# Slots of stationary activations and high weights start at different remainders of 256 bytes

## The chip, the cores and the metric

The kernel runs on one core of a Trainium2 chip. The metric is the device time of one execution in microseconds (us); the time before is the median of three runs. A core has TensorE (the matrix engine, PE in the profile; its weight loads are PEld), VectorE (DVE), ScalarE (ACT), GpSimd (POOL) and the queue of SyncE (SP). Operands of a matmul lie in SBUF, 128 partitions of some 224 KiB each; an address here is the byte offset within a partition. A matmul first loads its stationary operand (a weight load) and then streams its moving operand past it; the result goes to PSUM.

## The reference

One decoder block, all in float32, with 256 positions and a model width of 2048:

```python
a = rmsnorm(h, norm_mix_pre)
proj = a @ w_in                        # 2048 x 17408
q_a, k_a, v_a, q_r, f_r, i_r, g_r, gate_a, gate_r = split_columns(proj)
attn = ...   # rotary, three groups of dilated windowed attention, mixed by softmax of their log-sums
r_out = ...  # gated linear recurrence in chunks of 64, rmsnorm per head, silu(g_r)
y = sigmoid(gate_a) * (attn @ w_attn_branch) + sigmoid(gate_r) * (r_out @ w_hgrn_branch)
h = h + rmsnorm(y @ w_mix_out, norm_mix_post)
a = rmsnorm(h, norm_ffn_pre)
gt, up = split(a @ w_ffn_gate_up)      # 2048 x 11264
h = h + rmsnorm((silu(gt) * up) @ w_ffn_down, norm_ffn_post)   # 5632 x 2048
```

## The kernel before, in words

Float32 products are made from two-part numbers. Every weight tile is loaded into `raw`, split into a high part (`w`, rounded by ScalarE) and a low part (the rest, by VectorE), and every activation likewise; a product is the sum of high x high, high x low and low x high, each a matmul in the type fp32r. `split` (L282) and `split_wide` (L320) do this for weights, the class `Split` (L429) for activations.

Weights come in an order written out by hand: `seq` is a list of steps, grouped in blocks (L286 to L329), and the main loop (L343) takes one step at a time. It splits the weights of the step after next (`AHEAD` is 2), issues the load three units ahead on the SP queue (`load_behind`, L274), multiplies, and lets pieces of other work (evacuations, attention, recurrence) run between steps as generators. Operations stand on each engine in program order.

There are three kinds of blocks:

- "N" (`multiply`, L296): activations are stationary (128 x 128), 512 columns of weights move. One step has 12 matmuls: two halves of the positions, two row tiles, three products. High and low weights are the two halves of one `w` slot.
- "Wide" (`multiply_wide`, L351): the same roles, 1024 columns of weights per step and 24 matmuls, or, in steps marked 1 in the order, seven products of 2 x 2 blocks instead of eight, 21 matmuls, with sums of weights (`w`, `wl`, `dh`, `dl`) and sums of activations (`so`). Here the low weights have tiles of their own, `wl`.
- "W" (`multiply` too): weights are stationary, the activations xT move: the high weight against 512 columns (high and low part side by side), the low weight against 256. Used for the forget, query and attention projections.

Where operands lie: `rslot` (L110) hands out 16 slots of 1024 elements (4096 bytes) in turn, tag "r"; each holds two row tiles of an activation, high and low. xT, yT, hT, recT and attnT, the sums `so` and the split activations `a` of the last product live there. `wslot` (L279) hands out three slots of 2048 elements (8192 bytes), tag "w". All pool sizes in front of them are such that every one of these slots, and of `raw`, `wl`, `dh` and `dl`, begins at an address whose remainder by 256 is 192. Within a slot, stationary blocks begin at multiples of 512 bytes, moving ones in the "N" and "Wide" blocks at multiples of 2048.

SBUF is full: the last tile ends 64 bytes below 224 KiB. `kp` is a pool that lives through the early and the middle stage; `pool["now"]` is the pool of the present stage alone (early, middle, late; `enter`, L177). `gainr` (4 KiB, L202) is the gain of the recurrence's norm; it is loaded in `opening` (L582) and read by `evac_g` (L750) early on.

The spacing of matmuls comes from the one helper that issues them:

```python
    def mm(ps, lhsT, rhs, start, stop):
        nc.tensor.matmul(ps, lhsT, rhs, start=start, stop=stop, skip_group_check=True)
```

`lhsT` is the stationary operand and is loaded anew for each matmul; all of these matmuls have line L132 in the profile.

Of the kernel before, what the change touches and what calls it, by code (L numbers as in the profile page):

```python
# [13 lines left out]
F32 = mybir.dt.float32  # L14
F32R = mybir.dt.float32r
# [4 lines left out]
P = 128  # L20
# [6 lines left out]
HW = 1024  # L27
# [13 lines left out]
N_RAW, N_SPLIT, AHEAD, WARM, BRIDGE = 3, 3, 2, 8, 6  # L41
# [49 lines left out]
def tile_hybrid_block(ctx: ExitStack, tc: tile.TileContext, t, out):  # L91
# [4 lines left out]
    stream = ctx.enter_context(tc.tile_pool(name="stream", bufs=1, reuse_waits="tile"))  # L96
    rpool = ctx.enter_context(tc.tile_pool(name="rpool", bufs=1, reuse_waits="tile"))
# [3 lines left out]
    dram = ctx.enter_context(tc.tile_pool(name="dram", bufs=1, space=bass.MemoryType.DRAM))  # L101
    ctx.enter_context(tc.manual_schedule())

    serial = [0]

    def nm(s):
        serial[0] += 1
        return f"{s}_{serial[0]}"

    def rslot(s):  # L110
        return rpool.tile([P, 1024], F32R, tag="r", bufs=16, name=nm(s))

    def hslot(s):
        return hpool.tile([P, 2, 512], F32, tag="h", bufs=4, name=nm(s))
# [60 lines left out]
    pool = {}  # L175
# [13 lines left out]
    kp = stage.enter_context(tc.tile_pool(name="kp", bufs=1, reuse_waits="tile"))  # L189
# [9 lines left out]
    cs = kp.tile([P, 2, S], F32, name="cs")  # L199
    amask = kp.tile([P, 2, 512], F32, name="amask")  # L200
    lmask = kp.tile([P, len(LEVELS), 64], F32, name="lmask")
    gainr = kp.tile([P, HW], F32, name="gainr")  # L202
    tabs = kp.tile([P, 4, S], F32, name="tabs")
    bounds = kp.tile([P, 64], F32, name="bounds")
    lb, lb1 = bounds[:, :8], bounds[:, 8:16]


    blocks, seq, units = [], [], []

    def add(*args, **kw):  # L210
        b = Block(*args, **kw)
        blocks.append(b)
        for c in range(b.steps):
            if c % 2 == 0:
                units.append([])
            seq.append(Step(b, c, len(units) - 1, c % 2))
            units[-1].append(seq[-1])
# [59 lines left out]
            load(st.unit + N_RAW, half)  # L277

    def wslot():  # L279
        return stream.tile([P, 2048], F32R, tag="w", bufs=N_SPLIT, name=nm("w"))  # L280

    def split(st, only=None):  # L282
        if type(st.block) is Wide:
            split_wide(st)
            return
        raw = st.raw  # L286
        if st.parts is None:
            w = wslot()
            st.parts = w[:, :1024], w[:, 1024:]
        wh, wl = st.parts  # L290
        for n, k in enumerate(parts(st)):
            if only in (None, n):
                nc.scalar.activation(wh[:, k], raw[:, k], AF.Copy)  # L293
                nc.vector.tensor_sub(wl[:, k], raw[:, k], wh[:, k].bitcast(F32))  # L294
# [25 lines left out]
    def split_wide(st):  # L320

        b, raw = st.block, st.raw
        m, by7 = b.order[st.i]
        prep = b.prep(m, by7) if b.prep else iter(())
        next(prep, None)
        hi, lo = wslot(), p3("wl", F32R, 2048, 3)
        if not by7:
            nc.scalar.activation(hi, raw, AF.Copy)  # L328
            next(prep, None)  # L329
            nc.vector.tensor_sub(lo, raw, hi.bitcast(F32))  # L330
            st.parts = hi, lo
            return
        s, d = p3("sum", F32, 2048, 1), raw[:, 512:]
        nc.vector.tensor_sub(  # L334
            s[:, :1024].rearrange("p (a c) -> p a c", a=2),
            raw[:, 512:1536].rearrange("p (a c) -> p a c", a=2),
            raw[:, None, :512].to_broadcast([P, 2, 512]),
        )
        nc.scalar.activation(hi[:, :1024], s[:, :1024], AF.Copy)  # L339
        nc.vector.tensor_add(s[:, 1024:1536], raw[:, 512:1024], s[:, 512:1024])  # L340
        nc.vector.tensor_sub(s[:, 1536:], raw[:, 1536:], s[:, 1024:1536])
        nc.scalar.activation(hi[:, 1024:], s[:, 1024:], AF.Copy)  # L342
        next(prep, None)  # L343
        dhi, dlo = p3("dh", F32R, 1536, 1), p3("dl", F32R, 1536, 1)
        nc.scalar.activation(dhi, d, AF.Copy)  # L345
        nc.vector.tensor_sub(lo, s, hi.bitcast(F32))  # L346
        next(prep, None)
        nc.vector.tensor_sub(dlo, d, dhi.bitcast(F32))  # L348
        st.parts = hi, lo, dhi, dlo
# [79 lines left out]
    class Split:  # L429


        def __init__(self, s, nk, slot=rslot):
            self.flat = [slot(s) for _ in range(nk // 2)]
            self.slots = [x.rearrange("p (k z t) -> p k z t", k=2, z=2) for x in self.flat]
            self.there = set()
# [207 lines left out]
    def more_x(c):  # L643
        if c + 2 < KD // 2:
            transpose_in(xt, colg, xT, c + 2)
        else:
            lanes[1].append(pair_sums(xT, X7[c - 6 :: 2], x7, lambda: rslot("so")))
# [469 lines left out]
    def aslot(s):  # L1117

        x = rslot(s).bitcast(F32) if len(act_t) < 8 else p3(s, F32, 1024, 3)
        return x.rearrange("p (k t) -> p k t", k=4)  # L1120
# [197 lines left out]
    w = t["w_ffn_gate_up"][0]  # L1318
# [119 lines left out]
```

## Time and profile before

| what | value |
|---|---|
| median of 3 runs | 1722.73 us (1722.08 to 1725.4) |
| profiled execution, its own time | 1723.16 us |
| its span, first to last instruction | 1721.4 us |
| granted TensorE clock, mean | 0.998 |
| TensorE busy | 1705.4 us (99%) |
| weight loads busy | 1431.0 us (83%) |
| VectorE busy | 1356.9 us (79%) |
| ScalarE busy | 895.9 us (52%) |
| moved by DMA | 344.78 MB, 200 GB/s in the mean |

The profile comes from one execution. A line of the groups gives source line, engine, operation, output <- inputs, shape and count, then busy time and the mean duration of one in ns, then idle time before them. Matmuls are pipelined, so the duration of one (some 389 ns with 512 columns) holds its latency and overlaps the next; the pace is the distance between starts. In the chain of waits a line is start, length, what, and a count. In the windows the columns are window, length, and then busy time (and count) of PE, PEld, DVE, ACT and POOL, the granted clock, the share of the DMA engines and GB/s.

### The profile page before, as it was taken

The numbers are of one execution on the slowest core, as the hardware profiler recorded it, in microseconds if no ns is written. First come the engines' busy times: TensorE is split into PE (matmuls) and PEld (weight loads), VectorE is DVE, ScalarE is ACT, GpSimd is POOL, SyncE is SP. The second block draws the span as 40 slices with busy tenths as digits, with TensorE's granted clock in tenths as the row PEclk, the third lists the DMA queues.
The fourth block names the chain that finished last, engine by engine and source line by source line (L and its number), as shares of the span: only waits on it lengthen the run. The fifth ranks groups of instructions, "written<-read, shape, count | busy, mean of one in ns | idle before, by whom it ended". The sixth has DMA issues, their size and how long they took to land.

```text
span 1721.4 us, 21535 instructions
## 1 busy us (share of the span) xinstructions
PE 1705.4 (99%) x8357; PEld 1431.0 (83%) x8357; DVE 1356.9 (79%) x1477; ACT 895.9 (52%) x1007; POOL 21.7 (1%) x38
## 2 busy tenths in 40 slices
PE   9999999999999999999999999999999999999997
PEld 7788888888888898888888877888888888888886
DVE  6668888886677887777666578888888888898998
ACT  6545555554435434544444465555555555665663
POOL 0000000000000000000000000000000000000000
PEclk9999999999999999999999999999999999999999
DMA  7765666667544645565556745555555555666653
GB/s 253 272 220 208 232 231 221 220 226 251 185 158 159 220 159 172 173 206 167 164 172 202 245 163 196 196 195 196 197 201 201 203 201 201 217 198 217 201 197 116
DMA packets 208742, 344.78 MB, mean 200 GB/s; under 512 B 10960, under 2 KB 77696, under 8 KB 208640
## 3 DMA queue, kind: packets, MB, share of 16 engines
q1 hardware_dynamic: 198848, 319.41, 55.1%
q10 hardware_dynamic: 6880, 13.51, 2.1%
q0 software_dynamic: 2912, 10.49, 1.8%
q8 instruction: 65, 1.06, 0.2%
q14 instruction: 37, 0.30, 0.1%
HBM read 331.83 MB, written 11.53 MB: 199 GB/s over the span
## 4 chain that ended last, share of the span: by engine, by line
PE 96%; DVE 1%; ACT 1%; DMA 1%; issue 0%; SPq 0%; DVEq 0%; ACTq 0%
PE acc L132 62%; PE aux L132 33%; PE aux L491 0%; DVE w L294 0%; PE aux L817 0%; DMA gpost<-in_norm_mix_post 0%; PE acc L1131 0%; DVE fz L1258 0%; ACT w L293 0%; PE aux L1131 0%; PE aux L479 0%; ACT junk L1212 0%; DVE e L1208 0%; ACT junk L1105 0%; DVE wl L330 0%
## 5 line engine op out<-in xcount | busy, mean ns | idle before, releaser
L294 DVE TENSOR_TENSOR w<-raw,w 128x1024 fp32r<-128x1024 f32 (+1 forms) x225 | 274.1, 1219 | 188.0 <-ACT w L293 187.2
L293 ACT ACTIVATE w<-raw 128x1024 fp32r<-128x1024 f32 (+1 forms) x225 | 237.1, 1055 | 289.1 <-PE acc L132 250.2
L132 PE MATMUL acc<-xT,w 128*128 128x256 f32 (+1 forms) x2048 | 370.4, 339 | 0.0
L132 PEld LDWEIGHTS acc<-xT,w 128*128 128x128 f32 x2048 | 311.6, 188 | 43.3
L330 DVE TENSOR_TENSOR wl<-raw,w 128x2048 fp32r<-128x2048 f32 x125 | 285.8, 2287 | 63.4 <-ACT w L328 63.3
L328 ACT ACTIVATE w<-raw 128x2048 fp32r<-128x2048 f32 x125 | 238.8, 1911 | 133.8 <-PE aux L132 66.7
L346 DVE TENSOR_TENSOR wl<-sum,w 128x2048 fp32r<-128x2048 f32 x63 | 144.3, 2291 | 65.0 <-ACT w L342 63.9
L132 PE MATMUL acc<-w,hT 128*128 128x512 f32 x622 | 182.5, 392 | 1.5 <-DVE w L294 1.2
L132 PE MATMUL acc<-w,xT 128*128 128x512 f32 x536 | 157.3, 395 | 2.7 <-DVE w L294 1.5
L339 ACT ACTIVATE w<-sum 128x1024 fp32r<-128x1024 f32 x63 | 67.0, 1064 | 172.1 <-DVE sum L334 161.8
L132 PEld LDWEIGHTS acc<-w,hT 128*128 128x128 f32 x622 | 115.8, 188 | 27.0 <-DVE w L294 2.5
L132 PE MATMUL aux<-w,hT 128*128 128x512 f32 x430 | 135.6, 389 | 0.0
L132 PEld LDWEIGHTS acc<-w,xT 128*128 128x128 f32 x536 | 100.6, 189 | 24.9 <-DVE w L294 2.6
L132 PE MATMUL aux<-w,xT 128*128 128x512 f32 x386 | 121.1, 389 | 0.0
L348 DVE TENSOR_TENSOR dl<-raw,dh 128x1536 fp32r<-128x1536 f32 x63 | 110.4, 1752 | 0.0
L132 PEld LDWEIGHTS aux<-w,hT 128*128 128x128 f32 x430 | 80.7, 188 | 16.7
L345 ACT ACTIVATE dh<-raw 128x1536 fp32r<-128x1536 f32 x63 | 92.9, 1474 | 0.0
L132 PE MATMUL acc<-w,yT 128*128 128x512 f32 x384 | 88.2, 390 | 0.3 <-DVE w L294 0.3
L132 PEld LDWEIGHTS aux<-w,xT 128*128 128x128 f32 x386 | 72.6, 188 | 15.1
L132 PEld LDWEIGHTS acc<-w,yT 128*128 128x128 f32 x384 | 71.8, 188 | 15.5 <-DVE w L294 0.7
L132 PE MATMUL aux<-w,a 128*128 128x512 f32 x268 | 83.7, 389 | 0.0
L132 PE MATMUL acc<-w,a 128*128 128x512 f32 x268 | 83.7, 389 | 0.0
(258 smaller groups left out, 2654.4 us busy)
## 6 DMA issues: line engine op xcount, KB each, us to landing
raw<-in_w_in SPq DMA_DIRECT2D x271, 512.0 KB, 4.7
raw<-in_w_ffn_gate_up SPq DMA_DIRECT2D x176, 512.0 KB, 4.4
raw<-in_w_ffn_down SPq DMA_DIRECT2D x88, 512.0 KB, 4.8
raw<-in_w_mix_out SPq DMA_DIRECT2D x32, 512.0 KB, 5.0
kept<-e ACTq DMA_DIRECT2D x32, 256.0 KB, 4.5
raw<-in_w_hgrn_branch SPq DMA_DIRECT2D x16, 512.0 KB, 4.6
raw<-in_w_attn_branch SPq DMA_DIRECT2D x16, 512.0 KB, 4.6
v<-kept POOLq DMA_DIRECT2D x8, 512.0 KB, 6.4
```

The costliest lines, as they stand in the source:

```text
L132: nc.tensor.matmul(ps, lhsT, rhs, start=start, stop=stop, skip_group_check=True)
L293: nc.scalar.activation(wh[:, k], raw[:, k], AF.Copy)
L294: nc.vector.tensor_sub(wl[:, k], raw[:, k], wh[:, k].bitcast(F32))
L328: nc.scalar.activation(hi, raw, AF.Copy)
L330: nc.vector.tensor_sub(lo, raw, hi.bitcast(F32))
L339: nc.scalar.activation(hi[:, :1024], s[:, :1024], AF.Copy)
L345: nc.scalar.activation(dhi, d, AF.Copy)
L346: nc.vector.tensor_sub(lo, s, hi.bitcast(F32))
L348: nc.vector.tensor_sub(dlo, d, dhi.bitcast(F32))
```

## The change

An r slot is 1040 elements (4160 bytes) long instead of 1024, and of each eight consecutive slots the last four are used from 32 bytes in. A w slot is 2064 elements (8256 bytes) long, of which the first 2048 are used. A tile of 64 bytes, never used, is put into the pool in front of `raw` and `w`, and `gainr` goes from the long-lived pool to that of the early stage, whose space is given to others when the stage ends. With this, `raw` slots begin at remainder 0 of 256, `w` slots at 0, 64 and 128, and the eight slots of xT at eight different multiples of 32; `wl`, `dh`, `dl` and the tiles behind them stay at 192. No instruction is added, taken away or moved on any engine; a few waits on ScalarE and GpSimd refer to other earlier users of the same space.

```diff
-    serial = [0]
+    serial, slots = [0], [-1]
...
     def rslot(s):
-        return rpool.tile([P, 1024], F32R, tag="r", bufs=16, name=nm(s))
+
+        n = slots[0] = (slots[0] + 1) % 16
+        at = n // 4 % 2 * 8
+        return rpool.tile([P, 1040], F32R, tag="r", bufs=16, name=nm(s))[:, at : at + 1024]
...
-    gainr = kp.tile([P, HW], F32, name="gainr")
+    gainr = pool["now"].tile([P, HW], F32, name="gainr")
...
     blocks, seq, units = [], [], []
+    stream.tile([P, 16], F32, name="space")
...
     def wslot():
-        return stream.tile([P, 2048], F32R, tag="w", bufs=N_SPLIT, name=nm("w"))
+        return stream.tile([P, 2064], F32R, tag="w", bufs=N_SPLIT, name=nm("w"))[:, :2048]
```

## The prediction

> **What bounds the kernel now.** I read the page's engine totals first, then the chain of waits, then the matmuls by form.
>
> ```profile
> span 1721.4 us, 21535 instructions
> PE 1705.4 (99%) x8357; PEld 1431.0 (83%) x8357; DVE 1356.9 (79%) x1477; ACT 895.9 (52%) x1007; POOL 21.7 (1%) x38
> PEclk9999999999999999999999999999999999999999
> PE 96%; DVE 1%; ACT 1%; DMA 1%; issue 0%; SPq 0%; DVEq 0%; ACTq 0%
> q1 hardware_dynamic: 198848, 319.41, 55.1%
> ```
>
> TensorE is busy for 99% of the span at a full clock, 96% of the chain that ended last is TensorE, and the weight queue holds 55.1% of the DMA engines. So the time is the number of matmuls times the distance between their starts. An edit that leaves TensorE's list alone can move the time only through that distance.
>
> The chain of waits merges matmuls that follow one another; a piece's length over its count is the distance from start to start. These are from the stages in which a weight tile streams and activations stand still:
>
> ```profile
> 147.54 12.24 PE aux L132 x54
> 159.78 2.72 PE acc L132 x12
> 162.50 7.48 PE aux L132 x33
> 27.78 10.95 PE acc L132 x48
> 946.84 57.24 PE acc L132 x251
> 39.45 2.78 PE acc L132 x12
> ```
>
> 12.24 us over 54 is 226.7 ns; 2.72 over 12 and 7.48 over 33 give 226.7 again. In these pieces the stationary blocks begin 0, 512, 1024 or 1536 bytes into a slot and the moving ones 0, 2, 4 or 6 KiB, while slots and PSUM banks alternate; the spacing does not move. So what lies above 512 bytes of an address does not count. What lies below 256 bytes the trace cannot say: before the change every slot begins at remainder 192 of 256. The last row is a step behind four matmuls of another kind: 2.78 over 12, 231.7 ns, with the same shape and the same remainders. The spacing therefore is not a constant of the shape. It is 226.7 once the stream has settled, and about 5.0 ns more for about ten matmuls behind a disturbance (48 in 10.95 us, 228.1; 251 in 57.24 us, 228.0, between the two).
>
> How far above its floor is 226.7 ns? The nearest row with 512 columns and smaller operands is the warm-up, two bfloat16 matmuls whose weight loads and the load behind them the timeline shows:
>
> ```profile
> 7.38 0.10 PEld L132 LDWEIGHTS <-warm 128*128 128x128 bf16 x1
> 7.59 0.14 PEld L491 LDWEIGHTS aux<-ident,x 128*128 128x128 f32 x1
> ```
>
> The starts are 0.21 us apart, with both times rounded to 0.01; I use 0.215. So up to 11.7 ns of each 226.7 may be something other than streaming. That matmul also reads weights and moving columns at one remainder (it reads the tile `warm` for both), so bfloat16 shows no price for it; only the four-byte stream, which reads twice the bytes, could.
>
> The counts, from the matmuls by form (first and last of 36 rows with 512 columns in fp32, 6499 in all), and the weights-stationary stage in the chain of waits:
>
> ```profile
> L132 PE MATMUL acc<-xT,w 128*128 128x512 f32 x1024 | 334.9, 400 | 0.0
> L132 PE MATMUL acc<-xT,w 128*128 128x256 f32 x1024 | 201.5, 278 | 0.0
> L132 PE MATMUL acc<-dl,a 128*128 128x512 f32 x12 | 4.7, 389 | 0.0
> 456.72 11.16 PE acc L132 x64
> 454.93 1.78 PE aux L132 x16
> ```
>
> 6499 less the 1024 of the first row leaves 5475 matmuls in the activation-stationary stages. In the other stage weights stand still and xT moves: two of 512 and two of 256 columns take 11.16/64 x 4 = 697 ns. Its 256-column matmuls stand near the pace of weight loads alone (16 short matmuls in 1.78 us, 111 ns each), so little can come from them.
>
> **The change part by part.** *Sixteen r slots of 4160 instead of 4096 bytes, every other group of four entered 32 bytes in.* 4160 is 64 over a multiple of 256, so xT's eight tiles begin at eight different remainders, and hT's, yT's and the activations' likewise. *Three w slots of 8256 bytes* begin at 0, 64 and 128. `wl`, `dh` and `dl` keep 192. As slots turn, a moving and a stationary operand share a remainder in about one pair of eight. No instruction, transfer, operand size or wait on TensorE is added, and the order on every engine stays. Direct cost: nothing. Its effect is in the distance between starts alone, for 7/8 of the pairs.
>
> From above, the saving is the whole 11.7 ns on 5475 x 7/8 = 4791 matmuls, 56 us, with some 10 us more in the other stage. From below, it is a loss, priced under the second rival. Between them I take the row nearest in kind: the only variation of spacing that the same shape shows is 5.0 ns (231.7 against 226.7), so I take 5 ns as what a different relation of the two read streams is worth, and as a saving, because two streams that start together in the same place are the arrangement with most to lose. 4791 x 5 = 24.0 us; the 1024 wide matmuls of the other stage, by the same value, 1024 x 7/8 x 5 = 4.5 us. Sum 28.5 us.
>
> TensorE: Matmul & The Clock Gate in the Trainium skill (Wait — 56ns, not 53.3ns?) gives 215.7 ns between warm bfloat16 matmuls of 512 columns, which this trace's 0.21 agrees with; by that figure the whole excess would be 11.0 ns and the upper end 53 us.
>
> Is anything late once TensorE is 2% quicker? The windows show what feeds it:
>
> ```profile
> 106.00:330.00 224.00, 224.00 (x990) 185.49 (x989) 188.26 (x150) 124.50 (x103) 0.00 (x0) 1.00 0.65 226
> 1100.00:1460.00 360.00, 360.00 (x1627) 298.88 (x1626) 313.36 (x255) 195.65 (x163) 0.00 (x0) 1.00 0.56 196
> ```
>
> VectorE, the third pair of columns, holds 313 of 360 us (87%) in the feed-forward stage; at 353 us instead of 360 (5 ns on 7/8 of 226.7 ns spacings, 1.9%) it would be 89%, ScalarE 56%. Neither becomes the bound. If that cover were gone, the stage's gain would stop at VectorE's 313 us, which no case here reaches.
>
> *`gainr` in the early pool, the 64-byte tile `space`.* They make room and shift addresses.
>
> ```profile
> 41.51 0.47 SPq L582 DMA_DIRECT2D gainr<-in_hgrn_norm_gain  x1
> 396.25 2.02 PE L132 MATMUL acc<-xT,w 128*128 128x512 f32 x11
> L750 DVE TENSOR_TENSOR g<-sig,gainr x4: 691/692/693, 47.3 to 74.3; 128x512 f32<-128x512 f32 x4
> ```
>
> The tile is loaded at 41.5 us and read for the last time at 75 us; the middle pool that takes its place opens with the first weights-stationary block, at 396 us, so nobody waits for it: 0 us. With that cover gone a tile of the middle stage would wait for four VectorE reads of 0.69 us, under 3 us once. `raw` moves from remainder 192 to 0; transfers use 55% of the DMA engines and the chain holds 1% of DMA: 0 us either way. A few waits move on ScalarE (three) and on GpSimd's memset of `at`, all to work that was done long before.
>
> The sum against the profiled execution: 1723.16 - 28.5 = 1694.7, so 1695 us; that execution (1721.4 of span and 1.8 around it) is 0.4 us over the median of the runs shown, less than the sum can tell.
>
> **The rivals.** *Nothing happens.* The two reads of TensorE don't meet, or their meeting doesn't depend on addresses; the 11.7 ns is what a four-byte stream costs. For it: the spacing ignores every address bit that the trace varies. Against it: the spacing of one shape moves by 5 ns with the history of the stream, which a fixed cost would not do. Time: 1723 us. SBUF — State Buffer in the Trainium skill (Who interferes with whom) speaks for this one: it gives TensorE two independent read ports, one for the moving operand and one for LDWEIGHTS, and says that TensorE never waits on anyone.
>
> *The settled rhythm is lost.* The place is the border of each step. Before, all steps present the same remainders, so the stream settles once and keeps 226.7 through hundreds of matmuls. After, the pair of remainders changes with each step of 12 or 24 matmuls, and within a wide step between `w` and `wl`. If the rhythm has to be found anew each time, as behind other work (231.7 over the first twelve), most matmuls run unsettled: 5475 x 5.0 = 27 us, 1723.2 + 27.4 = 1751 us. The other stage, at 697 ns, never settled and stays. It decides from the point at which settling takes about as long as a step, and the last row of the first stretch says that it does. Against it: settling may be a matter of the order of instructions, not of addresses.
>
> *The change doesn't do what it says* is hardly open: the slot sizes alone set the remainders, and only 1 in 8 pairs stays equal by accident.
>
> **How the numbers follow.** Forecast 1695 us, chance 0.47; its own range reaches from nearly the full 66 us (1660) to 4 us (1719). No change, 0.20. Lost rhythm, 0.33, from 1727 to 1751. I lean to the gain because a price for equal remainders would be paid by every matmul before, and the excess over 0.215 us is just such a uniform price; I lean no further because the trace holds no matmul of this shape with other remainders. The range 1664 to 1750 leaves out the last 5 us of each sign, together about 0.12. A difference under 0.2% (3.4 us) is what a measurement of this kernel can't well tell from none; faster by more 0.47, within 0.20, slower by more 0.33.
>
> **What would show it.** Right: pieces of 54 matmuls in the stretch from 100 to 330 us shorter than 12.24 us, near 12.0, alike for `w` and `wl`; and the block of 64 under 11.16 us. No change: 12.24 and 2.72 again. Lost rhythm: steps of twelve at 2.75 us or more throughout, 11.16 as before. The forecast is wrong if spacing in the steady stretches stays at 226.7 or rises, or if TensorE gets shorter streams but idles before them.

## The result, and the profile after

The changed kernel takes 1750.61 us (median of 4 runs, 1750.17 to 1751.38) against 1723.59 us before: a ratio of 1.0157, 95% interval 1.0139 to 1.0174, so 27 us slower. The forecast of 1695 us was wrong in sign; the rival "the settled rhythm is lost" had 1751 us. Whether that rival's reason is the right one is what the experiments are for.

The page of the changed kernel, the lines that answer to those of before:

```profile
span 1749.6 us, 21535 instructions
PE 1732.3 (99%) x8356; PEld 1433.0 (82%) x8357; DVE 1356.9 (78%) x1477; ACT 897.3 (51%) x1007; POOL 21.7 (1%) x38
PEclk9999999999999999999999999999999999999999
PE 97%; ACT 1%; DVE 1%; DMA 1%; issue 0%; SPq 0%; DVEq 0%; ACTq 0%
L334 DVE TENSOR_TENSOR wl<-raw,w 128x2048 fp32r<-128x2048 f32 x125 | 285.8, 2288 | 85.2 <-ACT w L332 85.2
L332 ACT ACTIVATE w<-raw 128x2048 fp32r<-128x2048 f32 x125 | 239.2, 1914 | 155.9 <-PE aux L135 73.2
```

The instructions are the same in number, the clock is full, and VectorE's and ScalarE's commands last as long as before (the splits of a wide tile 2288 and 1914 ns, 2287 and 1911 before). TensorE's busy time grew by 27 us and is still 99% of the span: it does the same work at a slower pace. The chain of waits says where (start, length, what, count):

```profile
151.24 12.52 PE aux L135 x54
163.76 2.79 PE acc L135 x12
166.55 7.64 PE aux L135 x33
466.44 11.19 PE acc L135 x64
```

The piece of 54 takes 12.52 us instead of 12.24, 231.9 ns from start to start instead of 226.7; the pieces of 12 and 33 come to 232.5 and 231.5. The block of 64 of the weights-stationary stage has 11.19 us instead of 11.16. Over the whole trace the distance between starts of matmuls with 512 columns in the activation-stationary stages is 232.0 ns in the mean (some 5400 of them, those behind a wait left out), 226.9 before: 5.1 ns x 5400 = 27.5 us, and the spans differ by 28.2 us. So nearly the whole loss lies in the spacing of these matmuls.

### The profile page after: what moved, and what is told of

It reads as the page before. It is cut to its first block, busy times and chain, and to the rows that moved or that the text cites. A ratio compares the mean times of both kernels' runs of the same rounds, so it can differ in the third digit from the quotient of the medians.

```text
span 1749.6 us, 21535 instructions
## 1 busy us (share of the span) xinstructions
PE 1732.3 (99%) x8356; PEld 1433.0 (82%) x8357; DVE 1356.9 (78%) x1477; ACT 897.3 (51%) x1007; POOL 21.7 (1%) x38
## 4 chain that ended last, share of the span: by engine, by line
PE 97%; ACT 1%; DVE 1%; DMA 1%; issue 0%; SPq 0%; DVEq 0%; ACTq 0%
PE acc L135 63%; PE aux L135 33%; PE aux L821 0%; PE aux L495 0%; DVE w L298 0%; DMA x<-in_x 0%; PE acc L1135 0%; ACT w L297 0%; DMA cs<-in_rope 0%; PE aux L1135 0%; PE aux L483 0%; ACT junk L1109 0%; DVE fz L1262 0%; DVE wl L334 0%; ACT w L332 0%
## 5 line engine op out<-in xcount | busy, mean ns | idle before, releaser
L297 ACT ACTIVATE w<-raw 128x1024 fp32r<-128x1024 f32 (+1 forms) x225 | 237.1, 1056 | 293.1 <-PE acc L135 252.5
L334 DVE TENSOR_TENSOR wl<-raw,w 128x2048 fp32r<-128x2048 f32 x125 | 285.8, 2288 | 85.2 <-ACT w L332 85.2
L332 ACT ACTIVATE w<-raw 128x2048 fp32r<-128x2048 f32 x125 | 239.2, 1914 | 155.9 <-PE aux L135 73.2
```

## The experiments

Two theories stood. *Lost rhythm*: any lasting relation of the moving tile's remainder to the stationary slot's settles at 226.7 ns, and the loss comes from changing it at each step. *Own pace*: each relation has a pace of its own, and equal remainders happen to have the shortest. In what follows "offset" is the remainder by 256 of the moving tile's start less that of the stationary slot, in bytes (in the weights-stationary stage, of the stationary weight less that of the moving xT). All runs are compared with the kernel before on the same chip. Kernels 2, 3, 4, 7, 8, 9 and 10 have `gainr` and the small tile `ones` in the early pool, to make room, and these slots, whose starts all stay at 192:

```diff
+        o = off[0]
-        return stream.tile([P, 2048], F32R, tag="w", bufs=N_SPLIT, name=nm("w"))
+        return stream.tile([P, 2112], F32R, tag="w", bufs=N_SPLIT, name=nm("w"))[:, o : o + 2048]
...
-        hi, lo = wslot(), p3("wl", F32R, 2048, 3)
+        hi, lo = wslot(), p3("wl", F32R, 2112, 3)[:, o : o + 2048]
...
-        dhi, dlo = p3("dh", F32R, 1536, 1), p3("dl", F32R, 1536, 1)
+        dhi, dlo = (p3(x, F32R, 1600, 1)[:, o : o + 1536] for x in ("dh", "dl"))
```

They differ in how `off[0]` (in elements of 4 bytes) is set. TensorE's list is the same in all.

**1. The room that was made, alone.**

```diff
-    gainr = kp.tile([P, HW], F32, name="gainr")
+    gainr = pool["now"].tile([P, HW], F32, name="gainr")
...
+    stream.tile([P, 16], F32, name="space")
```

> Only gainr in the early pool and the 64-byte tile in front of raw are kept; every slot still begins at one common remainder (0 now, 192 before), so each stationary and moving operand of fp32r matmuls stays equal modulo 256. Both theories (lost rhythm; own pace for each relation) expect no change: 1723 us, ratio 1.000, pieces of 54 matmuls 12.24 us. If instead the shifted raw buffers or gainr's pool carry the loss: about 1751 us.

Measured: 1723.50 us against 1723.67, ratio 0.9999 (0.9990 to 1.0009).

```profile
147.33 12.24 PE aux L132 x54
159.57 2.72 PE acc L132 x12
```

Every slot of these operands now begins at remainder 0 instead of 192 and the pace is the old one. Neither `gainr`'s pool nor the place of `raw` costs anything, and of the two common remainders, 0 and 192, neither is better.

**2 and 3. One offset for the whole run, 64 and 32 bytes.** `off = [16]` and `off = [8]`.

> Every moving weight tile (w, wl, dh, dl) begins 64 bytes further in than the stationary slots, always the same: the difference stationary minus moving is 192 modulo 256 in the activation-stationary stages for the whole run, and 64 in the weights-stationary stage. Lost rhythm (a loss arises only where the relation changes): the stream settles as before, 1723 us, pieces of 54 in 12.24 us. Own pace for each relation (from the steps of twelve of the changed kernel with this difference, mean 228.9 ns after the first five): 2.2 ns on 5400 matmuls, 12 us, 1735 us, pieces of 54 near 12.36 us.

> The same with 32 bytes: the difference is 224 modulo 256 throughout the activation-stationary stages. Lost rhythm: 1723 us. Own pace (the changed kernel's steps with this difference have 233.4 ns after the first five): 6.7 ns on 5400 matmuls, 36 us, 1759 us, pieces of 54 near 12.60 us.

Measured: 1731.57 us with 64 bytes (1.0044, 1.0029 to 1.0059) and 1759.87 us with 32 (1.0207, 1.0192 to 1.0222). The chain of waits, first with 64 bytes, then with 32:

```profile
149.44 12.36 PE aux L132 x54
161.80 2.75 PE acc L132 x12
949.75 57.76 PE acc L132 x251
460.79 11.09 PE acc L132 x64
```

```profile
151.41 12.60 PE aux L132 x54
164.00 2.80 PE acc L132 x12
166.80 7.70 PE aux L132 x33
```

With 64 bytes the stream settles at 228.9 ns, with 32 at 233.3 (12.60/54, 2.80/12, 7.70/33), and piece after piece keeps that pace as it kept 226.7, though nothing in the relation ever changes. A pace is a mean: with 64 bytes the single distances in the trace repeat in threes, about 232, 226 and 229 ns. The constant offset of 32 is even slower than the change itself. This rejects lost rhythm as the only cause: a relation that never changes can be slow by itself. With 64 bytes the loss is 8 us and not 12, in part because the weights-stationary blocks got quicker: 11.09 us for 64 instead of 11.16.

**4 and 7. Sweeps.** The offset is constant in a block and grows from block to block of a kind, by 16 bytes and by 4:

```diff
+    def offset_of(b):
+        kind = "wide" if type(b) is Wide else b.kind
+        mine = [x for x in blocks if ("wide" if type(x) is Wide else x.kind) == kind]
+        return mine.index(b) % 16 * 4          # * 1 in the second sweep
+
     def split(st, only=None):
+        off[0] = offset_of(st.block)
```

> One look: the moving weight tiles' offset is constant within a block and grows by 16 bytes from block to block of a kind (0 to 240, then again). Lost rhythm: every block settles to 226.7 ns after its first dozen of matmuls, about 1725 us. Own pace: blocks differ, 226.7 at offset 0, 229 at 64, 233 at 32, 96 and 128; offsets that are odd multiples of 16 are unknown and may be better or worse than all of these; about 1750 us in all.

> One look: offsets of the moving weight tiles grow by 4 bytes from block to block of a kind (0 to 60). Own pace by 16-byte lines: offsets 0 to 12 behave alike (226.9), 16 to 28 near 231.7, 32 to 44 and 48 to 60 near 233.3. Own pace by single elements: offsets in between differ from these, and one of them may be below 226.7. Lost rhythm alone: all blocks near 226.9 (already against the run with 32 bytes throughout).

Measured, one run each: 1752.14 and 1752.45 us. The seven early wide blocks with pieces of 54 have the offsets 16, 32, 48, 64, 80, 96 and 112 in the first sweep:

```profile
106.95 12.51 PE acc L132 x54
149.34 12.59 PE aux L132 x54
192.03 12.59 PE acc L132 x54
234.72 12.37 PE aux L132 x54
276.62 12.47 PE acc L132 x54
318.90 12.61 PE aux L132 x54
361.62 12.47 PE acc L132 x54
```

and 4, 8, 12, 16, 20, 24 and 28 in the second:

```profile
107.37 12.83 PE acc L132 x54
150.76 12.61 PE aux L132 x54
193.46 12.37 PE acc L132 x54
235.36 12.51 PE aux L132 x54
277.75 12.96 PE acc L132 x54
321.67 12.64 PE aux L132 x54
364.45 12.32 PE acc L132 x54
```

Divided by 54: 231.7, 233.1, 233.1, 229.1, 230.9, 233.5, 230.9; and 237.6, 233.5, 229.1, 231.7, 240.0, 234.1, 228.1. The offset of 16, which the two sweeps have in different blocks, gives 12.51 us in both, and 32 and 64 give what they gave throughout a run (12.59 and 12.37 against 12.60 and 12.36): it is the offset that counts and not the block's place. The distances between starts over all activation-stationary matmuls of a sweep (each value from some 225 to 740 of them), in ns:

| offset, bytes | 0 | 32 | 64 | 96 | 128 | 160 | 192 | 224 |
|---|---|---|---|---|---|---|---|---|
| first sweep | 227.3 | 233.3 | 229.3 | 233.4 | 232.6 | 234.1 | 233.3 | 233.1 |

| offset, bytes | 16 | 48 | 80 | 112 | 144 | 176 | 208 | 240 |
|---|---|---|---|---|---|---|---|---|
| first sweep | 231.7 | 233.3 | 231.1 | 230.9 | 233.2 | 233.3 | 234.7 | 229.5 |

| offset, bytes | 4 | 8 | 12 | 20 | 28 | 36 | 44 | 60 |
|---|---|---|---|---|---|---|---|---|
| second sweep | 237.1 | 233.3 | 228.9 | 239.3 | 227.9 | 235.1 | 230.0 | 227.9 |

The other eight offsets of the second sweep lie between 227 and 235. So the mean pace goes with the offset, from 227.3 (equal starts, with the blocks' beginnings) to 239.3, and none of the offsets tried has a lower mean than equal starts. Single elements count, not only lines of 16 bytes: 4 bytes beside equal is among the worst. The eight multiples of 32, which the change brings about equally often, have 232.0 in the mean; the changed kernel's spacing is 232.0.

The offset alone does not fix the pace, though. Of a late wide block of the first sweep, with offset 240, the chain shows:

```profile
1374.54 11.20 PE acc L132 x48
1390.72 7.48 PE acc L132 x33
1400.92 7.48 PE acc L132 x33
```

The first 48 matmuls stand 233.3 ns apart; behind eight short matmuls of another kind the rest of the block stands 226.7 apart, the pace of equal starts, with nothing changed in the offset. The table's 229.5 is a mean over such stretches. What decides between the two is open.

**5 and 6. The parts of the change.** Only the r slots (`rslot` as in the change, `wslot` as before), and only the w slots (`wslot` and `space` as in the change, `rslot` as before); `gainr` is moved for room in both.

> The r slots as in the change (eight remainders), w, wl, dh and dl all at 192 as before. Lost rhythm (the loss comes from the relation's changing at each step): a stationary slot lasts 12 to 24 matmuls as in the change, about 1750 us. Own pace for each relation (from the sweep, offsets that are multiples of 32: 227.3, 233.3, 229.3, 233.4, 232.6, 234.1, 233.3, 233.1, mean 232.0): the eight relations come equally often, so 1750 us too. It says whether the stationary slots are enough for the whole loss.

> The w slots as in the change (0, 64, 128), the r slots, wl, dh and dl all at 192. Own pace: 3656 high and narrow-block matmuls have the offsets 64, 128 and 192 in turn (229.3, 232.6, 233.3, mean 231.7, against 226.9), the other 1819 stay equal: +17.5 us; the weights-stationary stage wins some 1 to 2 us; 1739 us. Lost rhythm: w and wl alternate within every wide step and w changes at each step, so nearly all 5400 matmuls are unsettled: about 1750 us.

Measured: r slots alone 1750.44 us (1.0156, 1.0140 to 1.0171), w slots alone 1745.28 us (1.0128, 1.0111 to 1.0144). The chain of waits of the second:

```profile
149.44 12.40 PE aux L132 x54
161.83 2.78 PE acc L132 x12
```

The r slots alone bring the whole loss, and both together no more: once the offsets are spread evenly, spreading them again changes nothing. Its trace also says why remainders by 256 are the measure: behind ten matmuls with one relation, those with 256 bytes between the starts stand 227.4 ns apart, those with 0 (by 512) 227.1. The second result lies between own pace (1739) and lost rhythm (1750), so own pace by itself is not enough either. In its trace the pairs that kept equal remainders (`wl`, `dh`, `dl`, 1807 of them) have 231.5 ns, not 226.9: a matmul's distance depends on its neighbours' offsets as well as on its own.

**8. One relation in each step, another in the next.**

```diff
     def split(st, only=None):
+        off[0] = 16 * (seq.index(st) % 2)
```

> Every moving weight tile alternates from step to step between offset 0 and offset 64, the stationary slots stay; within a step one relation holds. The constant forms of both are measured: 1723.5 and 1731.6 us. Own pace for each relation and nothing for the change between them: their mean, 1727.6 us. Lost rhythm on top (each change costs a new settling, as behind other work, some 5 ns on ten of 12 to 24 matmuls): 12 us or more above that, about 1740 to 1745 us.

Measured: 1735.21 us (1.0067, 1.0054 to 1.0081). The mean of its two constant forms is 1727.5 us (1723.50 and 1731.57). So the changing itself costs 7.7 us here, less than expected and clear of noise.

```profile
148.11 12.39 PE aux L132 x54
939.92 68.51 PE acc L132 x296
```

The constant forms have 12.24 and 12.36 for the piece of 54. In the "N" blocks, with steps of 12, the 296 matmuls stand 231.5 ns apart, while the constant forms have 228.0 (the same 57.24 us for 251 as before) and 230.1 (57.76): 2.4 ns above their mean. There, in the trace, a step with equal remainders starts with distances of 234, 231, 233, 236, 224, 231, 236, 228, 232, 231 and reaches 227 with the eleventh of its twelve matmuls, just as the stream does behind other work; that is some 50 ns more than ten settled distances. A step with 64 bytes needs only four (237, 235, 232, 232) before its three distances repeat, some 20 ns more than settled ones. So re-settling is real, too. One of the two relations settles sooner, which fits a cost below the 12 us expected.

**9 and 10. The other stage.** Equal starts are not the best in the weights-stationary stage: in the first sweep its 512-column matmuls stood 233.0 ns apart with offset 0 and 229.1 with 192. Number 9 sets 192 bytes in these blocks alone, number 10 sweeps from 160 to 220 in steps of 4 there, with offset 0 elsewhere.

```diff
     def split(st, only=None):
+        off[0] = 48 if type(st.block) is Block and st.block.kind == "W" else 0
```

> A version that may beat both: all relations equal as before in the activation-stationary stages; in the weights-stationary blocks alone the weights begin 192 bytes further in. Own pace (sweep: 512 columns 229.1 against 233.0 ns, 256 columns 116.3 against 115.9): about -3.9 x 1024 + 0.4 x 1024 ns = -3.6 us, 1720 us, ratio 0.998. If the sweep's difference was the blocks' position and not the offset: 1723.7 us.

> One look: as the last, with the weights' offset in the weights-stationary blocks from 160 to 220 bytes in steps of 4, constant within a block. Own pace: blocks differ by some ns per matmul, with 192 near 229 ns for 512 columns; 4 bytes beside it may be worse, as 4 bytes beside equal was (237 against 227) in the activation-stationary stages. About 1722 us.

Measured: number 9 1720.82 us against 1723.67, ratio 0.9981 (0.9972 to 0.9990), quicker than the kernel before by 2.9 us, and so than both. Number 10, one run: 1724.12 us.

```profile
148.91 12.24 PE aux L132 x54
457.53 11.06 PE acc L132 x64
```

The first row is that of the activation-stationary stage, unchanged; the second 11.06 us instead of 11.16. In number 10 the offset of 192 has 229.6 ns again and the others 231.1 to 237.5 (at 204), so among these offsets 192 is a narrow place and not the edge of a wide one.

## Why the prediction was wrong

*What bounds the kernel*: right. TensorE's list and the engines' durations stayed, and the time moved only through the spacing.

*The term of 5 ns*: right in size, wrong in sign, and this is the step that failed: the 24.0 us of saving were 27.5 us of loss, because the spacing rose by 5.1 ns. I took the 5 ns as a saving "because two streams that start together in the same place are the arrangement with most to lose". That was an analogy, without a row behind it. The constant offsets and the sweeps show the opposite: of the offsets tried, none has a shorter mean spacing than equal starts. That the size agrees is luck: 5.0 ns was what equal starts lose while they settle, 5.1 is the mean over eight relations whose own paces reach from 227.3 to 234.1. The 11.7 ns over the warm-up's 0.215 us, which I called a uniform price for equal remainders, was not won back by any offset tried: none settled below 226.7. Where those nanoseconds go stays open.

*The 4.5 us in the other stage*: not seen; a piece of 64 took 11.19 us against 11.16. Over the stage the 512-column matmuls got quicker, 231.7 against 233.3 ns, some 1.6 us for all 1024, but the 256-column ones, for which I had put down nothing, slower, 117.8 against 115.6 ns, some 2.2 us.

*The 7/8 of the pairs*: a wrong count for what followed. It counted which pairs change their own relation; number 6 shows that pairs which keep it lose as well, 231.5 against 226.9, when their neighbours differ. In the changed kernel's own trace the pairs with equal remainders have 231.1.

*The rival of the lost rhythm*: right in time (1751), partly by luck, since its 5.0 ns is again the settling of equal starts alone, and right in that changes cost a new settling (number 8: 7.7 us). It was wrong in holding that any lasting relation would settle at 226.7. Its sign, steps of twelve at 2.75 us or more, was seen (2.79), but a constant 32 bytes shows 2.80: that sign could not tell the two apart. A single offset of 32 bytes, never changed, costs 36 us, more than the change. In the changed kernel both are at work, and their shares can't be subtracted: the paces of the eight relations already have its mean, 232.0, and within its mixed stream good relations lose (equal starts 231.1) and bad ones gain (offset 160 has 232.8, against 234.1 in the sweep).

*Nothing happens*: rejected. SBUF — State Buffer in the Trainium skill (Who interferes with whom) gives TensorE two independent read ports and says that it never waits on anyone. Here the measurement decides against what I drew from it: 32 bytes between where the two operands start cost 2.07% of the time, with the same instructions. That the two reads meet is argued from this and not shown; the runs move the operands' starts, and which read waits for which they can't tell. Other engines' writes of the weights as the cause are made unlikely by number 5, which leaves every weight tile where it was and has the whole loss, and by the durations on VectorE and ScalarE, which did not move.

*TensorE: Matmul & The Clock Gate* in the Trainium skill (Wait — 56ns, not 53.3ns?) has 215.7 ns for such matmuls in bfloat16; no offset for the four-byte kind came nearer to it than the equal start's 226.7.

*`gainr`, `space`, `raw`*: right, 0 us (number 1). *The weights-stationary stage stays*: right for its sum in the change, and wrong as a general rule, since one lasting offset makes it quicker (11.06). *The other engines' cover*: not put to the test, as TensorE got no quicker; ScalarE's share there works out as 195.65 of 353 us, 55% and not 56.

*The range* reached to 1750 and the result is 1750.6. I had put its edge just inside the rival's 1751, 1 us and not "the last 5 us" of it, although that rival had a chance of 0.33 and its price stood as one number there; the edge belonged beyond that number.

## What to carry to other kernels

When TensorE sets the pace, look at the distance between starts, not at its busy share: a change without one new instruction cost 27 us through 5 ns per matmul. Before you spread buffers to avoid a conflict, try one lasting offset and a sweep by blocks in a single run; it shows each relation's pace in the chain of waits. Give an offset more than one block, since one can hold two paces. Keep the relation of stationary to moving starts the same across steps, and choose it by stage: the relation that is best where activations stand still (0) was not the best where weights do (192).

## What the runs showed of the hardware that was not expected

In the activation-stationary stages the pace of fp32r matmuls with 512 columns depends on where the moving tile starts relative to the stationary block: 226.7 ns with equal remainders, 228.9 with 64 bytes throughout, 233.3 with 32, 237 to 240 with 4 or 20. It depends on single elements of 4 bytes, and not on the common remainder (0 or 192). It has a memory: after a change of relation a stream with equal starts needs about ten matmuls to reach its pace, one with 64 bytes about four; a pair with equal remainders in a mixed stream has 231.5 ns; and one offset, 240, held 233.3 and 226.7 within a single block.
